# A two-layer encoder trunk (convolution, gated recurrence): small loads on GpSimd's queue or later, masks and lower bounds prepared in mid-run, first low parts on GpSimd

## The chip and the metric

One core of one Trainium2 chip. The metric is the device time of one execution in microseconds; the time before is 1019.38 us, the median of 3 runs (1018.51 to 1019.60). TensorE multiplies matrices, VectorE, ScalarE and GpSimd work on elements, and SyncE issues DMAs. Each engine works off its own queue in order; semaphores tie the queues together.

## What is computed

256 positions by 2048 channels, float32, two layers. Layer 0 is a gated convolution, layer 1 a bidirectional gated recurrence; both multiply their result by a gate and project it back.

```python
# layer 0
h = rms_norm(x, conv_norm)
a, b, z = split(h @ conv_w_in, 3)                    # w_in: 2048 x 6144
v = a * sigmoid(b)
v = depthwise_conv(v, conv_dw, width=31) + conv_dw_b
v = silu(layer_norm(v, conv_ln_g, conv_ln_b))
x = x + (v * silu(z)) @ conv_w_out                   # 2048 x 2048
# layer 1
h = rms_norm(x, hgrn_norm)
q, a_f, a_b, i, z = split(h @ hgrn_w_in, 5)          # 2048 x 10240
lb = cumsum(softmax(table over layers))              # one per direction; minus its first row
f = lb + (1 - lb) * sigmoid(a)                       # forget gate, k = (1 - lb) * sigmoid(-a)
o = forward and backward recurrence over 256 steps, 16 heads of 128
x = x + (rms_norm(o, o_norm) * silu(z)) @ hgrn_w_out
```

## The kernel before

**Weights.** Every product is done as three matmuls on a high and a low part of each operand (or two and a wide one): `hi*hi`, `hi*lo`, `lo*hi`. A list `plan` cuts the weights into blocks of 1 MB, 128 x 2048 values each. A block passes through three steps. `w_dma` (L109) loads it on SyncE's queue into one of 3 `raw` buffers; `w_split` (L122) lets ScalarE cast it to the high part `wh` (L134), and VectorE or GpSimd subtract that from `raw` to give the low part `wl` (L135); `w_next` (L139) hands it to the matmuls and keeps two splits and three loads ahead. There are 3 buffers of `wh` and `wl`. Blocks 0 to 47 are layer 0's input projection: blocks 0 to 7 are narrow (128 columns, all 2048 rows, a and b in turn for four column blocks), 8 to 31 are a and b of the column pairs 2 to 7, 32 to 47 are the gate z. The low part of blocks 4 to 47 is made by GpSimd, of all others by VectorE; blocks 0 to 3 are split in four pieces of 128x512.

**Start.** x is loaded, then one small vector, block 0 in four pieces, four vectors, block 1, five vectors, conv_dw (31 x 2048) and seven masks of 128 x 128, all on SyncE's queue (L256 to L276). The small ones land in `stage2`, as rows that TensorE transposes. ScalarE squares and sums x, VectorE makes a diagonal of the row norms, and `h0_gen` (L310) transposes and scales x by matmuls with that diagonal; `hilo` (L240) takes the high part on ScalarE and the low part on VectorE from PSUM. The 16 steps of `h0_gen` are interleaved with the first pass of matmuls (`pa` of block 0, L521). Behind that pass comes `vec_gen` (L335): it transposes the vectors and conv_dw, casts the masks to bytes, and computes the lower bounds `lb` and `oml = 1 - lb` of layer 1 in a chain of ten small VectorE operations with an exponential on ScalarE between them.

**Middle.** For each column pair `glu` multiplies a by the sigmoid of b on VectorE, then `conv_gen` (L404) runs 27 taps a block on VectorE and 4 on ScalarE and GpSimd, paced by estimated times against the matmuls (`run`, L233). `ln_gen` (L450) is the layer norm behind the last pair; the z blocks run beside it.

**Order.** What the program writes for one engine is ordered by a planner that simulates all engines: the instruction first in program order among those that it estimates to be ready goes first. So an instruction further down in the program can stand ahead of an earlier one in an engine's queue. The pool `pmm` has 4 slots of PSUM for the results of matmuls and for transposes.

Of the kernel before, what the change touches and what calls it, by code (L numbers as in the profile page):

```python
# [10 lines left out]
F32 = mybir.dt.float32  # L11
# [6 lines left out]
P = 128  # L18
S = 256
D = 2048  # L20
KB = D // P
CW = 31
# [6 lines left out]
NWD = D // WD  # L29
NKW = 4  # L30
AHEAD = 2
DV = 8
CHAIN0 = 2
ZPOS = 3
TK, TN = .654, .327
# [14 lines left out]
def trunk(ctx: ExitStack, tc: tile.TileContext, x, conv_norm, conv_w_in, conv_dw, conv_dw_b, conv_ln_g,  # L50
# [71 lines left out]
    def w_split():  # L122
        i = state["split"]
        if i >= len(plan):
            return
        raw = raws.pop(i)
        nk, ncol = raw.shape[1:]
        wh = wp.tile([P, nk, ncol], F32R, tag="wh", name=f"wh{i}", bufs=SPL + 1)
        wl = wp.tile([P, nk, ncol], F32R, tag="wl", name=f"wl{i}", bufs=SPL + 1)
        eng = G if 4 <= i < n_a and i % 8 != DV else V  # L130
        step = nk if i > 3 else 4
        for k in range(0, nk, step):
            sl = slice(k, k + step)
            A.copy(wh[:, sl, :], raw[:, sl, :])  # L134
            eng.tensor_tensor(out=wl[:, sl, :], in0=raw[:, sl, :], in1=wh[:, sl, :].bitcast(F32), op=ALU.subtract)  # L135
        splits[i] = (wh, wl)
        state["split"] = i + 1
# [95 lines left out]
    def run(gen, dt):  # L233
        for _ in gen:
            clock["pe"] += dt
            flush(clock["pe"])
            while bg and clock["bg"] <= clock["pe"]:
                clock["bg"] = max(clock["bg"], clock["pe"] - 2.0) + (pump() or clock["wait"])
# [22 lines left out]
    stage2 = big.tile([P, KB * S], F32, tag="yl", name="stage2")  # L261
    rows = stage2[:80, :2 * P].rearrange("q (a p) -> q a p", a=2)
    rows1, rows2 = rows[:, 0, :], rows[:65, 1, :]
    sync(rows1[:KB, :], conv_norm[0].rearrange("(a p) -> a p", p=P))
    w_dma()
    for i, v in enumerate((conv_dw_b[0], conv_ln_g[0], conv_ln_b[0], hgrn_norm[0])):
        sync(rows1[(i + 1) * KB:(i + 2) * KB, :], v.rearrange("(a p) -> a p", p=P))
    w_dma()
    for i, v in enumerate((lb_f[0], lb_b[0], lb_f[1], lb_b[1])):
        sync(rows2[i * KB:(i + 1) * KB, :], v.rearrange("(a p) -> a p", p=P))  # L270
    sync(rows2[64:65, :], o_norm)
    dwr = stage2[:CW, D:]
    sync(dwr, conv_dw[0])
    mask = cst.tile([P, len(LEVELS), P], U8, name="mask")
    mstage = stage2[:, 2 * P:(2 + len(LEVELS)) * P].rearrange("q (a p) -> q a p", p=P)
    sync(mstage, masks)  # L276

    ident = cst.tile([P, P], F32, name="ident")
    make_identity(nc, ident)
    ones = cst.tile([P, P], F32, name="ones")  # L280
    V.memset(ones, 1.0 / D)
    bcb = cst.tile([P, 1, S], F32, name="bcb")
# [49 lines left out]
    lb = cst.tile([P, 32], F32, name="lb")  # L332
    oml = cst.tile([P, 32], F32, name="oml")

    def vec_gen():  # L335
        tp = pmm.tile([P, 512], F32, tag="mm", name="tp_v1")
        nc.tensor.transpose(tp[:, :80], rows1, ident[:80, :80])
        nc.tensor.transpose(tp[:, 80:145], rows2, ident[:65, :65])
        V.tensor_copy(pvec[:, KB:], tp[:, KB:80])
        V.tensor_copy(pvec2, tp[:, 80:145])  # L340
        V.tensor_copy(mask, mstage)
        tp = pmm.tile([P, 512], F32, tag="mm", name="tp_dw")
        for k in range(KB):
            nc.tensor.transpose(tp[:, k * CW:(k + 1) * CW], dwr[:, k * P:(k + 1) * P], ident[:CW, :CW])
        V.tensor_copy(dw.rearrange("p k c -> p (k c)"), tp[:, :KB * CW])
        yield


        t0, t1 = pvec2[:, 0:32], pvec2[:, 32:64]
        lbw = cst.tile([P, 4, 32], F32, name="lbw")  # L350
        V.tensor_tensor(out=lbw[:, 0], in0=t0, in1=t1, op=ALU.max)
        V.tensor_tensor(out=lbw[:, 1], in0=t0, in1=lbw[:, 0], op=ALU.subtract)
        V.tensor_tensor(out=lbw[:, 2], in0=t1, in1=lbw[:, 0], op=ALU.subtract)
        A.activation(lbw[:, 1:3], lbw[:, 1:3], AF.Exp)
        V.tensor_tensor(out=lbw[:, 3], in0=lbw[:, 1], in1=lbw[:, 2], op=ALU.add)
        V.reciprocal(lbw[:, 3], lbw[:, 3])
        V.tensor_tensor(out=lbw[:, 1], in0=lbw[:, 1], in1=lbw[:, 3], op=ALU.mult)
        V.tensor_tensor(out=lbw[:, 2], in0=lbw[:, 2], in1=lbw[:, 3], op=ALU.mult)
        V.tensor_tensor(out=lb, in0=lbw[:, 1], in1=lbw[:, 2], op=ALU.add)
        V.tensor_tensor(out=lb, in0=lb, in1=lbw[:, 1], op=ALU.subtract)  # L360
        V.tensor_scalar(out=oml, in0=lb, scalar1=-1.0, scalar2=1.0, op0=ALU.mult, op1=ALU.add)
        yield


    yr = []
# [148 lines left out]
    for j in range(NCH):  # L514
        vb = vbuf[j % NV][:, :, PADW:PADW + S]
        sg = ca.tile([P, 2, S], F32, tag="sg", name=f"sg{j}", bufs=3)
        if j < NARROW:
            for u in range(2):
                pa = pmm.tile([P, S], F32, tag="mm", name=f"pa{j}_{u}")
                if j == 0 and u == 0:  # L520
                    for _ in ws_narrow(pa, hh, hl):  # L521
                        next(h0, None)
                    for _ in vec_gen():
                        pass
                else:
                    run(ws_narrow(pa, hh, hl), TN)
                pb = pmm.tile([P, S], F32, tag="mm", name=f"pb{j}_{u}")
                run(ws_narrow(pb, hh, hl), TN)
                A.activation(sg[:, u, :], pb, AF.Sigmoid)

                def glu(j=j, u=u, pa=pa, sg=sg, vb=vb):
# [17 lines left out]
                bg.append(ln_gen())  # L549

        later(LAG, glu)
    for j in range(NCH):
        pz = pmm.tile([P, 2, S], F32, tag="mm", name=f"pz{j}")
        run(ws_chunk(pz, hh, hl), TK)
# [288 lines left out]
```

## Time and profile before

| | us |
|---|---|
| median of 3 runs | 1019.38 |
| profiled execution | 1018.37 |
| its span, first to last instruction | 1016.6 |
| TensorE busy | 998.2 |
| VectorE busy | 753.7 |
| ScalarE busy | 511.3 |
| GpSimd busy | 243.8 |

An engine's busy time is what its instructions cover. Matmuls overlap: one of 256 columns lasts 0.28 us in the rows, and one starts every 0.12 us. A row of a view in order of time has the start in us from the start of the span, the busy time, the engine and line, the operation, `out<-in`, the shapes, a count where like ones were merged, and in brackets how long the engine stood idle ahead of it and who ended that. L12 is line 12 of the kernel. In the view by stretch each engine has its busy us and the number of its instructions; then come the granted clock, the mean busy share of the 16 DMA engines and GB/s. "Clock" is the granted clock of TensorE as a share of full speed.

### The profile page before, as it was taken

Reading aid. Unit: us, or ns where it says so; the run is one execution under the profiler, and the core shown is the slowest. Engines: PE = TensorE matmul, PEld = TensorE weight load, DVE = VectorE, ACT = ScalarE, POOL = GpSimd, SP = SyncE. Lnnn points to the kernel's source line nnn. Section 1 sums busy time; section 2 is a strip of 40 time slices with the busy share of each in tenths; the row PEclk is TensorE's granted clock in tenths of the full one; section 3 lists DMA queues with packets and bytes.
Section 4 is the critical chain, followed back from the end, with each engine's and each line's share of the span. In section 5 each row is a group of like instructions: output and inputs, shape, how many; then the busy total and the mean of one; then the engine's idle time right before and its main releaser. Section 6 shows DMA issues by size and latency. Waiting matters only on the chain.

```text
span 1016.6 us, 16064 instructions
## 1 busy us (share of the span) xinstructions
PE 998.2 (98%) x6625; PEld 883.9 (87%) x6625; DVE 753.7 (74%) x1214; ACT 511.3 (50%) x576; POOL 243.8 (24%) x99
## 2 busy tenths in 40 slices
PE   5999999999999999999999999999999999999998
PEld 5899999999997888888888888888888888887886
DVE  4687888888698655657877868778778786888552
ACT  6554554544565545454454555544555445454431
POOL 0399999999750000000000000000000000000000
PEclk9999999999999999999999999999999999999999
DMA  7755555555546555564454545555354555445461
GB/s 232 202 178 184 189 177 195 170 185 187 175 158 214 199 176 197 166 202 155 163 170 145 178 149 166 166 166 166 126 167 164 166 164 168 127 164 166 145 228 42
DMA packets 143995, 173.79 MB, mean 171 GB/s; under 512 B 2946, under 2 KB 109587, under 8 KB 143763
## 3 DMA queue, kind: packets, MB, share of 16 engines
q1 hardware_dynamic: 143922, 172.77, 52.4%
q8 instruction: 52, 0.85, 0.4%
q14 instruction: 21, 0.17, 0.0%
HBM read 170.66 MB, written 2.10 MB: 170 GB/s over the span
## 4 chain that ended last, share of the span: by engine, by line
PE 94%; DVE 2%; DMA 2%; SPq 1%; issue 0%; ACT 0%; DVEq 0%
PE psaf L172 6%; PE psab L172 6%; PE psq L172 6%; PE lv L682 4%; PE psab L174 3%; PE psaf L174 3%; PE psq L174 3%; PE psz L190 3%; PE pq L190 3%; PE psv L190 3%; PE po L191 3%; PE psv L191 3%; PE psz L191 3%; PE psz L192 3%; PE po L192 3%; PE psv L192 3%
## 5 line engine op out<-in xcount | busy, mean ns | idle before, releaser
L134 ACT CAST wh<-raw 128x2048 fp32r<-128x2048 f32 (+1 forms) x172 | 306.8, 1789 | 269.7 <-issue 52.6
L135 DVE TENSOR_TENSOR wl<-raw,wh 128x2048 fp32r<-128x2048 f32 (+1 forms) x128 | 266.8, 2090 | 114.2 <-ACT wh L134 112.6
L135 POOL TENSOR_TENSOR wl<-raw,wh 128x2048 fp32r<-128x2048 f32 x44 | 203.1, 4632 | 54.7 <-ACT wh L134 54.5
L426 DVE SCALAR_TENSOR_TENSOR acc<-vb,dw,acc 128x256 f32<-128x256 f32 x416 | 168.4, 481 | 12.0 <-ACT acc L401 10.7
L172 PE MATMUL psab<-hx,wh 128*128 128x512 f32 x256 | 92.8, 404 | 0.0
L172 PE MATMUL psaf<-hx,wh 128*128 128x512 f32 x256 | 92.8, 404 | 0.0
L172 PE MATMUL psq<-hx,wh 128*128 128x512 f32 x256 | 92.3, 402 | 0.0
L688 DVE TENSOR_TENSOR T<-T,pb 128x512 f32<-128x512 f32 x96 | 62.8, 686 | 15.9 <-PE lv L682 15.6
L158 PE MATMUL pz<-hx,wh 128*128 128x256 f32 x256 | 72.8, 285 | 0.0
L159 PE MATMUL pz<-hx,wh 128*128 128x256 f32 x256 | 72.7, 284 | 0.0
L160 PE MATMUL pz<-hx,wl 128*128 128x256 f32 x256 | 72.5, 283 | 0.0
L174 PE MATMUL psq<-hx,wl 128*128 128x256 f32 x256 | 72.2, 282 | 0.0
L174 PE MATMUL psab<-hx,wl 128*128 128x256 f32 x256 | 72.0, 281 | 0.0
L174 PE MATMUL psaf<-hx,wl 128*128 128x256 f32 x256 | 71.9, 281 | 0.0
L172 PEld LDWEIGHTS psaf<-hx,wh 128*128 128x128 f32 x256 | 48.1, 188 | 12.5
L172 PEld LDWEIGHTS psab<-hx,wh 128*128 128x128 f32 x256 | 48.1, 188 | 12.2
L172 PEld LDWEIGHTS psq<-hx,wh 128*128 128x128 f32 x256 | 48.1, 188 | 11.7
L662 ACT COPY kx<-T 128x512 f32<-128x512 f32 x56 | 37.0, 661 | 37.8 <-DVE T L688 37.7
L160 PE MATMUL pb<-hx,wl 128*128 128x256 f32 x192 | 54.4, 283 | 0.0
L158 PE MATMUL pa<-hx,wh 128*128 128x256 f32 x192 | 54.4, 283 | 0.0
L159 PE MATMUL pa<-hx,wh 128*128 128x256 f32 x192 | 54.4, 283 | 0.0
L158 PE MATMUL pb<-hx,wh 128*128 128x256 f32 x192 | 54.4, 283 | 0.0
(198 smaller groups left out, 2419.1 us busy)
## 6 DMA issues: line engine op xcount, KB each, us to landing
raw<-in_hgrn_w_in SPq DMA_DIRECT2D x80, 1024.0 KB, 5.1
raw<-in_conv_w_in SPq DMA_DIRECT2D x47, 1024.0 KB, 5.3
raw<-in_conv_w_out SPq DMA_DIRECT2D x16, 1024.0 KB, 5.2
raw<-in_hgrn_w_out SPq DMA_DIRECT2D x16, 1024.0 KB, 5.2
out<-ot SPq DMA_DIRECT2D x8, 256.0 KB, 2.4
xt<-in_x SPq DMA_DIRECT2D x1, 1024.0 KB, 5.1
xt<-in_x SPq DMA_DIRECT2D x2, 512.0 KB
raw<-in_conv_w_in SPq DMA_DIRECT2D x4, 256.0 KB, 7.9
```

What stands on the lines that cost most here:

```text
L134: A.copy(wh[:, sl, :], raw[:, sl, :])
L135: eng.tensor_tensor(out=wl[:, sl, :], in0=raw[:, sl, :], in1=wh[:, sl, :].bitcast(F32), op=ALU.subtract)
L158: mm(ps[:, j, :], lhsT=a, rhs=hi[:, k, :], start=(k == 0 and j == 0), stop=False)
L159: mm(ps[:, j, :], lhsT=a, rhs=lo[:, k, :], start=False, stop=False)
L160: mm(ps[:, j, :], lhsT=wl[:, kk, j * P:(j + 1) * P], rhs=hi[:, k, :], start=False, stop=(k == KB - 1 and j == 1))
L172: mm(ps[j].rearrange("p a s -> p (a s)"), lhsT=wh[:, kk, j * P:(j + 1) * P], rhs=hx[:, k].rearrange("p a s -> p (a s)"), start=(k == 0), s ...
L174: mm(ps[j][:, 0, :], lhsT=wl[:, kk, j * P:(j + 1) * P], rhs=hx[:, k, 0, :], start=False, stop=(k == KB - 1))
L190: mm(ps[t], lhsT=a, rhs=wh[:, kk, :], start=(k == 0), stop=False)
L191: mm(ps[t], lhsT=a, rhs=wl[:, kk, :], start=False, stop=False)
L192: mm(ps[t], lhsT=lo[:, k, t * P:(t + 1) * P], rhs=wh[:, kk, :], start=False, stop=(k == KB - 1))
L426: ins = V.scalar_tensor_tensor(out=accs[j, u], in0=vb[:, u, c:c + S], scalar=dw[:, k, c:c + 1], in1=accs[j, u], op0=ALU.mult, op1=ALU.add)
L688: V.tensor_tensor(out=tv, in0=tv, in1=pv, op=ALU.mult)
```

## The change

The loads of conv_norm, conv_dw, conv_dw_b, conv_ln_g, conv_ln_b and hgrn_norm are issued from GpSimd's queue, after the identity matrix is made there; on SyncE's queue blocks 0 and 1 follow x directly. The tables of the lower bounds, o_norm and the masks stay on SyncE, but are issued in the program behind the first pass, when the loads up to block 5 are written. `vec_gen` is cut in two: `vec_conv` (vectors of layer 0, conv_dw) is called behind the matmuls of block 1, `vec_rec` (masks, lower bounds) ahead of the z blocks. The low parts of the first two pieces of block 0 and of blocks 1 to 3 go to GpSimd. `DV` goes; its test was always true.

```diff
--- before.py
+++ after.py
@@ -29,7 +29,6 @@
 NWD = D // WD
 NKW = 4
 AHEAD = 2
-DV = 8
 CHAIN0 = 2
 ZPOS = 3
 TK, TN = .654, .327
@@ -127,10 +126,10 @@
         nk, ncol = raw.shape[1:]
         wh = wp.tile([P, nk, ncol], F32R, tag="wh", name=f"wh{i}", bufs=SPL + 1)
         wl = wp.tile([P, nk, ncol], F32R, tag="wl", name=f"wl{i}", bufs=SPL + 1)
-        eng = G if 4 <= i < n_a and i % 8 != DV else V
         step = nk if i > 3 else 4
         for k in range(0, nk, step):
             sl = slice(k, k + step)
+            eng = G if i < n_a and (i > 0 or k < 2 * step) else V
             A.copy(wh[:, sl, :], raw[:, sl, :])
             eng.tensor_tensor(out=wl[:, sl, :], in0=raw[:, sl, :], in1=wh[:, sl, :].bitcast(F32), op=ALU.subtract)
         splits[i] = (wh, wl)
@@ -261,22 +260,25 @@
     stage2 = big.tile([P, KB * S], F32, tag="yl", name="stage2")
     rows = stage2[:80, :2 * P].rearrange("q (a p) -> q a p", a=2)
     rows1, rows2 = rows[:, 0, :], rows[:65, 1, :]
-    sync(rows1[:KB, :], conv_norm[0].rearrange("(a p) -> a p", p=P))
-    w_dma()
-    for i, v in enumerate((conv_dw_b[0], conv_ln_g[0], conv_ln_b[0], hgrn_norm[0])):
-        sync(rows1[(i + 1) * KB:(i + 2) * KB, :], v.rearrange("(a p) -> a p", p=P))
-    w_dma()
-    for i, v in enumerate((lb_f[0], lb_b[0], lb_f[1], lb_b[1])):
-        sync(rows2[i * KB:(i + 1) * KB, :], v.rearrange("(a p) -> a p", p=P))
-    sync(rows2[64:65, :], o_norm)
-    dwr = stage2[:CW, D:]
-    sync(dwr, conv_dw[0])
     mask = cst.tile([P, len(LEVELS), P], U8, name="mask")
     mstage = stage2[:, 2 * P:(2 + len(LEVELS)) * P].rearrange("q (a p) -> q a p", p=P)
-    sync(mstage, masks)
-
+    dwr = stage2[:CW, D:]
+    small = G.dma_start
     ident = cst.tile([P, P], F32, name="ident")
     make_identity(nc, ident)
+    small(rows1[:KB, :], conv_norm[0].rearrange("(a p) -> a p", p=P))
+    w_dma()
+    w_dma()
+    small(dwr, conv_dw[0])
+    for i, v in enumerate((conv_dw_b[0], conv_ln_g[0], conv_ln_b[0], hgrn_norm[0])):
+        small(rows1[(i + 1) * KB:(i + 2) * KB, :], v.rearrange("(a p) -> a p", p=P))
+
+    def late_loads():
+        for i, v in enumerate((lb_f[0], lb_b[0], lb_f[1], lb_b[1])):
+            sync(rows2[i * KB:(i + 1) * KB, :], v.rearrange("(a p) -> a p", p=P))
+        sync(rows2[64:65, :], o_norm)
+        sync(mstage, masks)
+
     ones = cst.tile([P, P], F32, name="ones")
     V.memset(ones, 1.0 / D)
     bcb = cst.tile([P, 1, S], F32, name="bcb")
@@ -332,18 +334,20 @@
     lb = cst.tile([P, 32], F32, name="lb")
     oml = cst.tile([P, 32], F32, name="oml")
 
-    def vec_gen():
+    def vec_conv():
         tp = pmm.tile([P, 512], F32, tag="mm", name="tp_v1")
         nc.tensor.transpose(tp[:, :80], rows1, ident[:80, :80])
-        nc.tensor.transpose(tp[:, 80:145], rows2, ident[:65, :65])
         V.tensor_copy(pvec[:, KB:], tp[:, KB:80])
-        V.tensor_copy(pvec2, tp[:, 80:145])
-        V.tensor_copy(mask, mstage)
         tp = pmm.tile([P, 512], F32, tag="mm", name="tp_dw")
         for k in range(KB):
             nc.tensor.transpose(tp[:, k * CW:(k + 1) * CW], dwr[:, k * P:(k + 1) * P], ident[:CW, :CW])
         V.tensor_copy(dw.rearrange("p k c -> p (k c)"), tp[:, :KB * CW])
-        yield
+
+    def vec_rec():
+        tp = pmm.tile([P, 512], F32, tag="mm", name="tp_v2")
+        nc.tensor.transpose(tp[:, :65], rows2, ident[:65, :65])
+        V.tensor_copy(pvec2, tp[:, :65])
+        V.tensor_copy(mask, mstage)
 
 
         t0, t1 = pvec2[:, 0:32], pvec2[:, 32:64]
@@ -359,7 +363,6 @@
         V.tensor_tensor(out=lb, in0=lbw[:, 1], in1=lbw[:, 2], op=ALU.add)
         V.tensor_tensor(out=lb, in0=lb, in1=lbw[:, 1], op=ALU.subtract)
         V.tensor_scalar(out=oml, in0=lb, scalar1=-1.0, scalar2=1.0, op0=ALU.mult, op1=ALU.add)
-        yield
 
 
     yr = []
@@ -520,12 +523,13 @@
                 if j == 0 and u == 0:
                     for _ in ws_narrow(pa, hh, hl):
                         next(h0, None)
-                    for _ in vec_gen():
-                        pass
+                    late_loads()
                 else:
                     run(ws_narrow(pa, hh, hl), TN)
                 pb = pmm.tile([P, S], F32, tag="mm", name=f"pb{j}_{u}")
                 run(ws_narrow(pb, hh, hl), TN)
+                if j == 0 and u == 0:
+                    vec_conv()
                 A.activation(sg[:, u, :], pb, AF.Sigmoid)
 
                 def glu(j=j, u=u, pa=pa, sg=sg, vb=vb):
@@ -549,6 +553,7 @@
                 bg.append(ln_gen())
 
         later(LAG, glu)
+    vec_rec()
     for j in range(NCH):
         pz = pmm.tile([P, 2, S], F32, tag="mm", name=f"pz{j}")
         run(ws_chunk(pz, hh, hl), TK)
```

## Rows read from the trace of the kernel before

**Rows 1.** busy by stretch: stretch, length, PE, PEld, DVE, ACT, POOL, clock, DMA, GB/s
```profile
22.00:26.50 4.50, 4.31 (x36) 4.31 (x37) 2.76 (x7) 1.96 (x5) 0.00 (x0) 1.00 0.10 31
26.50:31.10 4.60, 2.24 (x21) 1.68 (x19) 1.48 (x6) 0.80 (x2) 0.00 (x0) 0.99 0.22 64
31.10:35.00 3.90, 3.90 (x22) 3.84 (x22) 2.75 (x7) 2.05 (x4) 0.00 (x0) 0.57 1.17 306
...
60.00:250.00 190.00, 190.00 (x1586) 190.00 (x1585) 160.61 (x401) 98.00 (x114) 188.75 (x72) 1.00 0.57 183
```

**Rows 2.** order of time, VectorE, start: start us, busy us, what [idle before]
```profile
24.60 0.48 DVE L242 SCALAR_TENSOR_TENSOR hx<-tp,pvec,hx 128x256 fp32r<-128x256 f32 x1 [0.66 <-ACT hx L241]
25.63 0.48 DVE L242 SCALAR_TENSOR_TENSOR hx<-tp,pvec,hx 128x256 fp32r<-128x256 f32 x1 [0.54 <-ACT hx L241]
29.54 0.63 DVE L341 CAST mask<-stage 128x896 uint8<-128x896 f32 x1 [3.42 <-DMA stage<-in_masks]
...
31.10 0.49 DVE L242 SCALAR_TENSOR_TENSOR hx<-tp,pvec,hx 128x256 fp32r<-128x256 f32 x1
...
32.20 0.18 DVE L352 TENSOR_TENSOR lbw<-pvec,lbw 128x32 f32<-128x32 f32 x1
...
33.60 2.50 DVE L135 TENSOR_TENSOR wl<-raw,wh 128x512 fp32r<-128x512 f32 x4 [1.12 <-ACT wh L134]
```

**Rows 3.** order of time, SyncE's queue, two issues
```profile
14.69 0.22 SPq L273 DMA_DIRECT2D stage<-in_conv_dw  x1
...
17.27 12.05 SPq L118 DMA_DIRECT2D raw<-in_conv_w_in  x1
```

**Rows 4.** order of time, ScalarE, two casts of weights
```profile
32.95 2.18 ACT L134 CAST wh<-raw 128x512 fp32r<-128x512 f32 x4 [1.89 <-DMA raw<-in_conv_w_in]
...
40.41 1.90 ACT L134 CAST wh<-raw 128x2048 fp32r<-128x2048 f32 x1
```

**Rows 5.** order of time, GpSimd, from its first low part on
```profile
42.39 4.63 POOL L135 TENSOR_TENSOR wl<-raw,wh 128x2048 fp32r<-128x2048 f32 x1 [40.79 <-ACT wh L134]
...
104.00 1.32 POOL L415 TENSOR_TENSOR prods<-prods 128x512 f32<-128x512 f32 x1
...
211.95 13.80 POOL L135 TENSOR_TENSOR wl<-raw,wh 128x2048 fp32r<-128x2048 f32 x3
...
235.77 4.61 POOL L135 TENSOR_TENSOR wl<-raw,wh 128x2048 fp32r<-128x2048 f32 x1
...
285.18 4.75 POOL L135 TENSOR_TENSOR wl<-raw,wh 128x2048 fp32r<-128x2048 f32 x1 [1.11 <-ACT wh L134]
```

**Rows 6.** order of time, TensorE, first passes and block 37
```profile
29.02 0.86 PE L344 MATMUL tp_dw<-ident,stage 31*128 31x31 f32 x11
...
31.50 0.58 PE L198 MATMUL pb<-hx,wh 128*128 128x256 f32 x1
...
34.23 0.39 PE L198 MATMUL pb<-hx,wh 128*128 128x256 f32 x1
...
39.02 0.28 PE L198 MATMUL pa<-hx,wh 128*128 128x256 f32 x1
...
240.62 0.28 PE L158 MATMUL pz<-hx,wh 128*128 128x256 f32 x1
```

**Rows 7.** waits of TensorE: us in total, times, longest
```profile
PE tp_v L293 <- DMA stage<-in_conv_norm: 9.8, 1, 9.8
```

**Rows 8.** order of time, VectorE, around and after pair 7's gate
```profile
214.66 0.69 DVE L545 TENSOR_TENSOR vb<-pa,sg 128x512 f32<-128x512 f32 x1 [2.72 <-ACT sg L542]
...
231.63 7.15 DVE L426 SCALAR_TENSOR_TENSOR acc<-vb,dw,acc 128x256 f32<-128x256 f32 x18 [2.42 <-ACT acc L401]
...
257.71 1.88 DVE L468 TENSOR_TENSOR y<-y,mu_ps 128x512 f32<-128x512 f32 x3 [4.03 <-PE mu_ps L454]
...
285.98 4.10 DVE L498 TENSOR_SCALAR y<-y,pvec 128x256 f32<-128x256 f32 x1
...
291.20 0.40 DVE L498 TENSOR_SCALAR y<-y,pvec 128x256 f32<-128x256 f32 x1
```

## The prediction

> **What bounds the kernel now.** I read the busy table by stretch first. From 60 to 250 us TensorE is busy 190.00 of 190.00 us, one matmul every 0.12 us (190.00 over 1586), at full clock [rows 1]; no edit can help there except by not hurting. What is left to win is at the start: in 26.50 to 31.10 TensorE is busy 2.24 of 4.60 us, and from 31.10 to 35.00 the granted clock is 0.57 of full speed, the lower of its two levels for most of it [rows 1]. Then I asked who holds TensorE there. VectorE's order of time [rows 2] shows it: it ends a low part at 26.11, then sits 3.42 us for the mask DMA, casts the mask at 29.54, and only then makes the last two low parts of the normalised input, the second at 31.10. The mask is not needed before layer 1; it stands in an in-order queue ahead of what TensorE needs. The third view is SyncE's queue and the DMA share [rows 3, 1]: conv_dw, 31 rows of 2048 values (248 KB), is issued at 14.69, and from 22.00 to 26.50 the 16 DMA engines are busy 0.10, near one engine of 16 (0.06). SyncE hangs 12.05 us in one weight issue from 17.27, and ScalarE waits for weight block 2 until 32.95 [rows 4]. One long-running transfer on about one engine holds up masks and weights behind it.
>
> A second limit hides under TensorE's: in 60 to 250 GpSimd is busy 188.75 of 190.00 [rows 1]. Its low part of block 4 starts at 42.39, that of block 37 ends at 240.38 (235.77 plus 4.61) [rows 5], and TensorE begins block 37 at 240.62, 35 blocks of 5.76 after block 2 at 39.02 [rows 6]. So GpSimd is 0.2 us ahead there (0.5 to the first matmul that takes the low part), and whatever makes it late shows as TensorE idle.
>
> **The change part by part.** I measure the start by when TensorE begins block 2, 39.02 now [rows 6].
>
> (a) Masks and bounds leave the start. The last low parts follow each other by 1.03 us (24.60 to 25.63) [rows 2]. Without the mask the last would end at 25.63 + 2 x 1.03 + 0.48 = 28.2 instead of 31.10 + 0.49 = 31.6: minus 3.4 us.
>
> (b) If the gap goes, so does the clock's drop: the 13 matmuls between 31.50 and 34.23 take 2.73 us [rows 6], at 0.12 each 1.56: minus 1.2. If a gap of like size stays elsewhere: 0.
>
> (c) The 17 transposes of the first vectors and of conv_dw now run in TensorE's gaps; they move behind pb of block 1, where no gap covers them. Eleven take 0.86, a step of 0.064 [rows 6]: plus 1.1. At best they fill gaps again: 0.
>
> (d) Weight block 2 comes earlier, because SyncE no longer passes conv_dw and the small vectors ahead of it. Its four casts (2.18 on ScalarE [rows 4]) can then go ahead of remaining high parts: 0 to plus 2.2, I take plus 1.1. Four low parts of a block leave VectorE (2.50 [rows 2]), which mattered only where VectorE held ScalarE up: 0 to minus 2.5, taken minus 0.6.
>
> (e) The PSUM slots of the two transposed vector tiles no longer stand between the first pass and the second, so matmuls of pb whose inputs are there may fill gaps: 0 to minus 4.3 (36 x 0.12); I take minus 1.5, a third of it, since the first pass leaves little room while it runs (TensorE busy 4.31 of 4.50 from 22.00 to 26.50 [rows 1]).
>
> Sum at the start: minus 3.4, 1.2, 0.6, 1.5, plus 1.1, 1.1: minus 4.5.
>
> (f) Six vectors go through GpSimd's queue. The trace has no such issue. The gain norm came through SyncE in time for TensorE to transpose it after a wait of 9.8 us from the start [rows 7]; it is needed by the first high part right behind the first casts. Below: an instant landing gains nothing, the square sums hold the start. Above: if it took as long as the longest issue of the start, 12.05 [rows 3], it would land near 14 and cost about 4. I take 0, by the nearest row, the same vector through SyncE. The five others are needed after block 1 only. SyncE's six late loads stand behind the weight issues up to block 5 and ahead of block 6, which TensorE wants only four blocks (23 us) after block 2; hidden, unless SyncE hangs again.
>
> (g) GpSimd takes 14 low parts of 128x512. Its add of that size takes 1.32 [rows 5], so 18.5 us in all, in a stretch where it does nothing now (it starts at 42.39). When does it reach block 4? If the casts of block 2 come only after the last high part, near 28.8, then 8 x 1.32 more make 39.5; if earlier, the cast of block 4 sets it, now at 40.41 [rows 4], then 4.5 earlier: 37.8 at its end. So block 4 starts 2.9 to 4.6 earlier; I take 3.8. With the 0.5 of lead, the later stretch can give TensorE 4.2 of its 4.5. If GpSimd were late here, all that is lost, one for one.
>
> (h) The moved preparation now stands in VectorE's queue just before the gate of block pair 7 (now 214.66), while GpSimd has low parts back to back. What this costs is shown by a row: at 285.98 the scale-and-shift of line 498, 0.40 when alone, takes 4.10 and ends at 290.08, as GpSimd's low part ends (285.18 + 4.75 = 289.93) [rows 8, 5]; 2 other such waits end the same way. So VectorE's tensor_scalar between SBUF tiles waits out a whole GpSimd instruction. Two of the moved operations are of like kind, SBUF to SBUF with one input: mask cast and oml. Each may wait 0 to 4.6, and the ten small ones at 0.18 [rows 2] and the cast at 0.63 add 2.5. Against 2.5 + 4.6 VectorE has idle 2.72 before that gate, 2.42 at 231.63 and 4.03 before 257.71 [rows 8]: most of it is covered. But the gate comes some 3.6 late, and behind it in ScalarE's queue stand a tap start, products and a weight cast that feeds GpSimd, whose lead is 0.2 to 0.5. I take plus 1.0, from 0 (covered) to 3. The two table loads that the exponential needs on ScalarE move there too; ScalarE is busy 98.00 of 190.00 [rows 1], no charge.
>
> A rule speaks against (h). The Trainium skill's page "SBUF — State Buffer", section "Who interferes with whom", says that a VectorE instruction in a two-port mode, or with two SBUF inputs while GpSimd reads SBUF, and a GpSimd instruction exclude each other for the whole instruction. The trace agrees for line 498; it has no case with two SBUF inputs. By it eight more of the moved operations would wait, which is the third rival.
>
> Total: minus 4.2 plus 1.0 is minus 3.2 on the profiled execution's 1018.37 (span 1016.6 and 1.8 around it): 1015.2. The median of the three runs, 1019.38, is 1.0 above that execution, so I state 1016.2.
>
> **The rivals.**
> 1. The start gives more: pb fills every gap (e at 4.3) and block 2 is cast early, block 4 starts at 36, (h) is covered. Gain 6 to 7: 1012.5. For it: DMA engines idle from 22 us on. Against: GpSimd's 0.2 us lead.
> 2. conv_dw clogs again. Now it goes out some 10 us earlier. If it again runs on about one engine, it shares that engine with x and the first weight blocks: 248 KB at one engine's share take about 10 us, half of it beside them. The first low parts then wait 2 to 4 us and eat most of (a): 1018.5 to 1020. For it: the 0.10 in rows 1. Against: another queue may spread it. The "DMA: Bandwidth & Descriptors" page of the Trainium skill (section "Why a DMA increments its semaphore by 16 and not by 1") says that GpSimd's queue gives some copies all 16 engines although 16 does not divide their rows; no run here shows that.
> 3. The other side: VectorE is blocked between GpSimd's low parts. Place: 212 to 240. If the mask cast, three small operations ahead of the exponential, and six behind it each wait for a GpSimd instruction, the first alone waits until 216.6 and the next until 221.3 (three low parts of 4.6 from 211.95 [rows 5]); the gate of pair 7 slips from 214.66 to about 222, and the weight cast behind it in ScalarE's queue with it. Then GpSimd itself starves, which lets the rest through. Low part 35, which now ends at 225.75 and is wanted at 229.1 (39.02 + 33 x 5.76), ends some 5.4 later, 2.0 too late, and 36 another 3: 5 us of TensorE idle, up to 12 if the second group is blocked as well, of which I take 6.5. That gives 1018.37 - 4.2 + 6.5 + 1.0 = 1021.7. It decides once the gate is later than about 220. For it: GpSimd's 188.75 of 190.00. Against: two-input operations are not seen to wait.
> 4. It does not do what it says: TensorE's start is held by the chain of high and low parts anyway (1.03 a step), (d) and (c) take what (a) gives, and (h) takes the rest: 1019.
>
> **How the numbers follow.** Forecast 0.44 (own range 1013.5 to 1018.5), rival 1 0.12, rival 2 0.10, rival 3 0.26, rival 4 0.08. 0.2% is 2.0 us, about what a measurement of this kernel can tell: faster is below 1017.4, slower above 1021.4. Faster: two thirds of the forecast (0.29), rival 1 and 0.01 of rival 2, 0.42. Slower: the upper part of rival 3 (0.20) and 0.04 of the others, 0.24. The same: 0.34. The range 1012 to 1023 leaves out a tenth at either end.
>
> **What would show it.** (a), (b): no VectorE wait for masks before 40 us, full clock at 31 to 35, block 2 begun near 34.5 instead of 39.02. (d): ScalarE not waiting for block 2. (f): conv_norm transposed by about 9.8. (g): GpSimd at block 4 near 38.5. (h): mask cast and oml longer than alone, and TensorE's idle from 212 to 260. I am wrong if TensorE begins block 2 later than 38, or if it idles more than 4 us between 212 and 260, or if the 128x512 low part on GpSimd takes far more than 1.32.

## The result and the profile after

The changed kernel takes 1024.19 us, the median of 5 runs (1023.29 to 1025.40); the kernel before, run beside it, 1018.97. The ratio is 1.0053, with a 95% interval of 1.0042 to 1.0065: slower by 5 us, where a gain of 3 was forecast. The profiled execution after took 1023.29, 4.9 us more than the one before (1018.37).

The view by stretch, of the same stretches of the start and of three in the middle (columns as in [rows 1]):

```profile
22.00:26.50 4.50, 2.64 (x20) 2.25 (x20) 2.20 (x5) 3.64 (x8) 4.50 (x5) 1.00 0.62 151
26.50:31.10 4.60, 4.60 (x39) 4.38 (x38) 1.93 (x4) 1.89 (x4) 3.52 (x3) 1.00 0.78 216
31.10:35.00 3.90, 3.90 (x33) 3.84 (x32) 0.49 (x2) 2.66 (x5) 1.56 (x2) 1.00 1.00 269
220.00:230.00 10.00, 9.80 (x82) 9.60 (x80) 10.00 (x18) 7.49 (x12) 5.95 (x2) 1.00 0.48 157
230.00:240.00 10.00, 7.18 (x55) 6.98 (x56) 10.00 (x26) 4.36 (x5) 9.84 (x6) 0.97 0.33 107
240.00:250.00 10.00, 10.00 (x75) 10.00 (x75) 10.00 (x26) 4.28 (x4) 9.92 (x5) 0.86 0.64 210
```

The hole from 26.50 to 31.10 and the fall of the clock behind it are gone, the DMA engines carry 0.62 where they carried 0.10 [rows 1]. But a hole has come at 22.00 to 26.50, and from 220 to 250, where TensorE had no gap, 212 matmuls ran in 30 us, where [rows 1] has 1586 in 190, about 250 in 30. In the last two of these stretches the granted clock is 0.97 and 0.86 besides. TensorE's waits name both places (us in total, times, longest; `hx` is the normalised input, `wl` a low part of the weights):

```profile
PE tp_v L295 <- DMA stage<-in_conv_norm: 7.9, 1, 7.9
PE tp L320 <- DVE diag L310: 3.8, 2, 1.9
PE pz L159 <- POOL wl L134: 3.0, 2, 2.5
PE pa L197 <- ACT hx L240: 1.7, 1, 1.7
...
PE pa L197 <- DVE pvec L340: 0.8, 1, 0.8
```

Where block 2 begins, in TensorE's order of time (the first row is for a comparison below):

```profile
27.16 1.05 PE L320 MATMUL tp<-diag,xt 128*128 128x128 f32 x8
...
39.13 0.38 PE L197 MATMUL pa<-hx,wh 128*128 128x256 f32 x1 [0.83 <-DVE pvec L340]
```

39.13 against 39.02 [rows 6]: the start has gained nothing. VectorE in order of time, three rows of the start and five of the middle:

```profile
12.97 1.00 DVE L310 TENSOR_SCALAR diag<-ident,ss 128x128 f32<-128x128 f32 x1
...
31.64 0.48 DVE L241 SCALAR_TENSOR_TENSOR hx<-tp,pvec,hx 128x256 fp32r<-128x256 f32 x1 [0.54 <-ACT hx L240]
37.31 1.63 DVE L350 CAST mask<-stage 128x896 uint8<-128x896 f32 x1 [5.18 <-DMA stage<-in_masks]
...
212.80 4.26 DVE L355 TENSOR_TENSOR lbw<-pvec 128x32 f32<-128x32 f32 x1
...
217.37 4.26 DVE L356 TENSOR_TENSOR lbw<-pvec,lbw 128x32 f32<-128x32 f32 x1
...
222.05 0.68 DVE L549 TENSOR_TENSOR vb<-pa,sg 128x512 f32<-128x512 f32 x1
...
225.59 0.18 DVE L364 TENSOR_TENSOR lb<-lb,lbw 128x32 f32<-128x32 f32 x1
...
226.08 4.22 DVE L365 TENSOR_SCALAR oml<-lb 128x32 f32<-128x32 f32 x1
```

The same small operation lasts 4.26 or 0.18. The gate of pair 7 stands behind two of the long ones, at 222.05 instead of 214.66 [rows 8]. GpSimd and ScalarE in order of time:

```profile
12.62 2.49 POOL L134 TENSOR_TENSOR wl<-raw,wh 128x512 fp32r<-128x512 f32 x2 [7.45 <-ACT wh L133]
...
39.05 4.62 POOL L134 TENSOR_TENSOR wl<-raw,wh 128x2048 fp32r<-128x2048 f32 x1 [0.60 <-ACT wh L133]
...
212.38 9.21 POOL L134 TENSOR_TENSOR wl<-raw,wh 128x2048 fp32r<-128x2048 f32 x2
225.64 4.62 POOL L134 TENSOR_TENSOR wl<-raw,wh 128x2048 fp32r<-128x2048 f32 x1 [4.05 <-ACT wh L133]
```
```profile
10.88 1.06 ACT L306 ACTIVATE stage<-xt 128x1024 f32<-128x1024 f32 x1 [1.51 <-DMA xt<-in_x]
...
15.28 0.47 ACT L240 ACTIVATE hx<-tp,pvec 128x256 fp32r<-128x256 f32 x1 [1.31 <-PE tp L320]
...
22.63 2.17 ACT L133 CAST wh<-raw 128x512 fp32r<-128x512 f32 x4
...
221.77 0.26 ACT L358 ACTIVATE lbw<-lbw 128x64 f32<-128x64 f32 x1 [5.93 <-DVE lbw L357]
...
223.67 1.89 ACT L133 CAST wh<-raw 128x2048 fp32r<-128x2048 f32 x1
```

Lay the rows over each other. GpSimd's two low parts from 212.38 end near 217.0 and 221.6. VectorE's two long operations end at 217.06 and 221.63, `oml` at 230.30 with GpSimd's next one (225.64 + 4.62 = 230.26). The six operations between them, at 0.18, fall into the 4.05 us in which GpSimd waits for ScalarE's cast. That cast, at 223.67, stands in ScalarE's queue behind the exponential of the chain, for which ScalarE sat idle 5.93 us until 221.77, and behind the first tap, which needs the late gate. So GpSimd starves, and TensorE waits 0.5 and 2.5 us for its low parts.

### The profile page after: what moved, and what is told of

The parts are those of the page before. It is cut to its first block, busy times and chain, and to the rows that moved or that the text cites. A ratio compares the mean times of both kernels' runs of the same rounds, so it can differ in the third digit from the quotient of the medians.

```text
span 1021.5 us, 16074 instructions
## 1 busy us (share of the span) xinstructions
PE 998.8 (98%) x6625; PEld 884.6 (87%) x6625; DVE 760.0 (74%) x1200; ACT 512.1 (50%) x577; POOL 265.0 (26%) x119
## 4 chain that ended last, share of the span: by engine, by line
PE 92%; DVE 3%; DMA 1%; ACT 1%; POOL 1%; issue 1%; SPq 0%; DVEq 0%; POOLq 0%; ACTq 0%
PE psaf L171 6%; PE psab L171 6%; PE psq L171 6%; PE lv L687 4%; PE psab L173 3%; PE psq L173 3%; PE psaf L173 3%; PE psz L189 3%; PE pq L189 3%; PE psv L189 3%; PE psv L190 3%; PE po L190 3%; PE psz L190 3%; PE psz L191 3%; PE po L191 3%; PE pq L190 3%
## 5 line engine op out<-in xcount | busy, mean ns | idle before, releaser
L134 DVE TENSOR_TENSOR wl<-raw,wh 128x2048 fp32r<-128x2048 f32 (+1 forms) x114 | 258.7, 2270 | 112.6 <-ACT wh L133 111.1
L134 POOL TENSOR_TENSOR wl<-raw,wh 128x2048 fp32r<-128x2048 f32 (+1 forms) x58 | 220.7, 3825 | 38.2 <-ACT wh L133 38.2
L159 PE MATMUL pa<-hx,wl 128*128 128x256 f32 x192 | 54.3, 283 | 0.0
```

The source lines that it names most:

```text
L159: mm(ps[:, j, :], lhsT=wl[:, kk, j * P:(j + 1) * P], rhs=hi[:, k, :], start=False, stop=(k == KB - 1 and j == 1))
```

## The experiments

Each was timed beside the kernel before, on one chip; 1 to 4, 5 to 8, 9 to 12 and 13 to 14 ran on four different chips, so across these groups the ratios are to be compared and not the us. "Block 2" is its first matmul in TensorE's order of time, in one profiled execution; before it is 39.02, after 39.13. The rows of the table are experiments 1 to 14.

| kernel | block 2 | us | ratio, 95% interval |
|---|---|---|---|
| change, chain of bounds in PSUM | 40.38 | 1018.81 | 1.0006 [0.9997, 1.0015] |
| before, preparation moved | 39.38 | 1022.98 | 1.0043 [1.0031, 1.0056] |
| change, conv_dw later | 38.65 | 1023.47 | 1.0048 [1.0034, 1.0061] |
| change, first low parts on VectorE | 40.41 | 1024.42 | 1.0053 [1.0040, 1.0065] |
| PSUM chain, mask cast on ScalarE | 40.40 | 1019.19 | 1.0005 [0.9996, 1.0014] |
| ... and block 0 and block 2's split mended | 36.83 | 1015.84 | 0.9977 [0.9968, 0.9986] |
| ... and conv_dw later: **all repairs** | 35.70 | 1014.65 | 0.9969 [0.9956, 0.9981] |
| before, preparation moved, PSUM, mask on ScalarE | 41.00 | 1019.42 | 1.0010 [1.0001, 1.0019] |
| all, block 0's low parts shared again | 36.16 | 1016.05 | 0.9979 [0.9970, 0.9988] |
| all, block 2 split early again | 36.96 | 1016.30 | 0.9980 [0.9971, 0.9989] |
| all, mask cast on VectorE again | 35.92 | 1014.93 | 0.9967 [0.9954, 0.9979] |
| all, small loads on SyncE's queue again | 40.73 | 1019.89 | 1.0015 [1.0006, 1.0023] |
| all, chain in SBUF again | 36.12 | 1020.30 | 1.0018 [1.0009, 1.0027] |
| all, blocks 1 to 3 on VectorE too | 38.00 | 1017.24 | 0.9994 [0.9985, 1.0003] |

The profiled executions fall into two groups. Take from each its time less the place of its block 2: before it is 1018.37 less 39.02, 979.35, after 1023.29 less 39.13, 984.16. The five kernels whose chain of bounds runs in the middle with its operands in SBUF (after, 2, 3, 4 and 13) have 983.9 to 984.8. The eleven others, before among them, have 978.9 to 979.4. So the start and the chain are two separate terms, and in these kernels the end moves by as much as block 2 does.

**1. The chain of bounds with at most one input in SBUF.** The operations stay where they are; one operand of each is kept in the PSUM tile of the transpose.

```diff
-V.tensor_tensor(out=lbw[:, 0], in0=t0, in1=t1, op=ALU.max)
+q = [tp[:, 128 + 32 * i:160 + 32 * i] for i in range(6)]
+V.tensor_tensor(out=q[0], in0=tp[:, 0:32], in1=t1, op=ALU.max)
...
-V.tensor_scalar(out=oml, in0=lb, ...)
+V.tensor_scalar(out=oml, in0=q[5], ...)
```

> The changed kernel, with the chain of the lower bounds kept partly in PSUM: every small VectorE operation of it has at most one SBUF input, and none goes from SBUF to SBUF. Place, order, exponential and table loads stay. Theory 1 (VectorE and GpSimd exclude each other where VectorE has two SBUF inputs or a scale-and-shift between SBUF tiles): the three operations of 4.2 us fall to 0.2, the gate of pair 7 comes back from 222.05 to about 215 to 217, TensorE's idle and slow clock between 220 and 250 (some 46 matmuls, 5.5 us) goes: 1018.5 to 1019.5. Theory 2 (the place costs it: ScalarE's queue held by the exponential and two table loads, whatever VectorE reads): 1023 to 1024.5.

VectorE in order of time, and the stretch around it (columns as in [rows 1]: GpSimd is busy 9.92 of 10.00 us):

```profile
214.07 0.19 DVE L357 TENSOR_TENSOR tp_v<-tp_v,pvec 128x32 f32<-128x32 f32 x1
...
215.84 0.69 DVE L553 TENSOR_TENSOR vb<-pa,sg 128x512 f32<-128x512 f32 x1 [0.61 <-ACT sg L550]
...
221.14 0.18 DVE L369 TENSOR_SCALAR oml<-tp_v 128x32 f32<-128x32 f32 x1
```
```profile
210.00:220.00 10.00, 10.00 (x86) 10.00 (x85) 8.08 (x26) 5.21 (x7) 9.92 (x5) 1.00 0.40 118
```

The same operations, with one copy more on VectorE and one on ScalarE, at the same place beside the same busy GpSimd, take 0.18 to 0.19 each (the reciprocal 0.35); TensorE waits for no low part there, and the time falls by 0.0047, 4.8 us. It is the place of the operands and not the work, nor the exponential and its table loads, which stayed (theory 2 is out). This kernel began block 2 at 40.38, 1.25 later than the change, with the same program there; see the last section.

**2. Before, with only the preparation moved.**

```diff
-        nc.tensor.transpose(tp[:, 80:145], rows2, ident[:65, :65])
-        V.tensor_copy(pvec2, tp[:, 80:145])
-        V.tensor_copy(mask, mstage)
+    vec_rec()                       # ahead of the z blocks, as in the change
```

> The kernel before, with one part of the change alone: the preparation for layer 1 is called ahead of the z blocks; all loads and all low parts stay as before. Theory 1: the same three waits of about 4.2 us stand between 212 and 231, 5 to 5.5 us are lost there, and the start changes by less than 1: 1023 to 1025. Rival (the loss of the change is bound up with the new start, for instance GpSimd's extra low parts that bring it late into the middle): 1017 to 1019.5.

```profile
212.97 4.28 DVE L353 TENSOR_TENSOR lbw<-pvec 128x32 f32<-128x32 f32 x1
...
226.27 4.22 DVE L363 TENSOR_SCALAR oml<-lb 128x32 f32<-128x32 f32 x1
```

VectorE's order of time shows the same stalls, TensorE's waits 3.1 us for GpSimd's low parts. This one edit makes the kernel before 1.0043 times as long: nearly the whole loss of the change. TensorE's clock stayed at 1.00 from 220 to 250 here, so the loss does not need the lower clock.

**3. The start: conv_dw later.** Its load is made to wait until x has been squared (a copy of 31 x 2 of the sums into its landing place); the four vectors behind it in the program have no such wait.

```diff
-    small(dwr, conv_dw[0])
+    A.copy(stage2[:CW, D - 1:D + 1], ss0[:CW, 1:3])
+    small(stage2[:CW, D:], conv_dw[0])
```

> The changed kernel, with conv_dw and four vectors held back on GpSimd's queue until x has been squared. Theory 3 (the start gives nothing because conv_dw now shares the DMA engines with x, so that the last half of x comes at 10.88 instead of 9.46): first high part near 14 instead of 15.28, block 2 begun 1 to 1.7 us earlier, 1022.5 to 1023.3. Rival (x is late for another reason, or the casts of block 2 and the mask hold the start anyway): 1024.

ScalarE, then VectorE:

```profile
9.22 1.06 ACT L303 ACTIVATE stage<-xt 128x1024 f32<-128x1024 f32 x1
```
```profile
12.04 2.35 DVE L311 TENSOR_SCALAR diag<-ident,ss 128x128 f32<-128x128 f32 x1
```

x is there 1.7 us earlier than in the change (10.88), so conv_dw's load beside x had cost that much. But the second diagonal matrix, a tensor_scalar from SBUF to SBUF, now falls under GpSimd's first two low parts as a whole and takes 2.35 where it took 0.29 before, so the first high part comes at 15.70, later than in the change. One repair uncovers the next; 0.5 us is left at block 2, less than expected, and the time does not tell the two kernels apart.

**4. The start: the first low parts on VectorE.**

```diff
-            eng = G if i < n_a and (i > 0 or k < 2 * step) else V
+            eng = G if 4 <= i < n_a else V
```

> The changed kernel, with the low parts of blocks 0 to 3 back on VectorE. Theory 3: GpSimd's low parts cost only the wait of the second diagonal (1.00 instead of 0.29), VectorE gets 14 x 0.62 us of work back between the low parts of the input: 1024 to 1026. Rival (GpSimd's first low parts hold the start up): 1021 to 1023.

```profile
13.81 0.28 DVE L310 TENSOR_SCALAR diag<-ident,ss 128x128 f32<-128x128 f32 x1
```

The diagonal matrix takes 0.28 again, but it begins at 13.81 instead of 12.97, behind two low parts of block 0 on VectorE, and is ready no earlier: 14.09 against 13.97. The first high part comes at 15.40 (15.28 in the change). Block 2 begins at 40.41, but TensorE's clock was low in this start (0.70 from 25 to 30), as in experiment 1. So the 1.28 between the two is not the price of the low parts; 14 has that on a start at full clock. No gain: the interval is that of the change.

**5. The masks' cast on ScalarE (with the chain in PSUM).**

```diff
-        V.tensor_copy(mask, mstage)
+        A.copy(mask, mstage)
```

> The kernel with the lower bounds' chain in PSUM, and besides the cast of the masks to bytes on ScalarE in place of VectorE. Theory A (the start lost part of its gain to the cast of the masks, which waits on VectorE for a low part on GpSimd and holds up the copy of the vectors' transpose behind it): block 2 begins 0.8 us earlier than with the cast on VectorE, TensorE waits for no copy of pvec there, and the time is about 0.8 us under the PSUM kernel's, some 1.000 of before. Rival B (the start is bound by the chain of x, its transposes and block 1's casts, and the cast stands beside it): block 2 begins no earlier, ratio 1.0005 as with the bounds in PSUM alone.

Block 2 at 40.40 against 40.38, ratio as in 1: no gain, as the rival had it. But the kernel of 1 does not show the wait of 0.83 us that the change has: its start was later by the low clock, and when TensorE came to block 2 the copy was already done. So this run can't price the cast's place; 11 has it on a start at full clock.

**6. Block 0 and block 2's split.**

```diff
-            eng = G if i < n_a and (i > 0 or k < 2 * step) else V
+            eng = G if 0 < i < n_a else V
...
-        while state["split"] < min(len(plan), i + 1 + SPL):
+        far = i + 1 + SPL - (i == 0)      # the loads likewise: far + RAW
+        while state["split"] < min(len(plan), far):
```

> As the one before, and besides all four low parts of block 0 on VectorE (blocks 1 to 3 stay on GpSimd), and block 2's split is begun with block 1's use, not with block 0's. Theory A: the second diagonal matrix takes 0.3 us in place of 1.0, as GpSimd's low parts begin after it; block 2's casts no longer stand ahead of half of the high parts; together 1 to 2 us less at the start than with the masks' cast moved alone: block 2 begins at 36.5 to 38, ratio 0.998 to 0.999. Rival B: the four low parts on VectorE stand ahead of its own low parts of x and give back what the diagonal matrix gains, block 2 begins at 38 to 39.5, ratio about 1.000.

Both edits together: block 2 at 36.83, ratio 0.9977, so rival B's time is out. Its mechanism is there all the same: the diagonal matrix stands behind two low parts on VectorE, begins at 13.97, and the first high part comes at 15.57 (15.31 in 5). By the rows the gain is the split's: block 2's casts stand between the high parts, TensorE's wait of 1.8 us for a high part is gone, and with it the low clock. Of the 3.57 us, about 1.25 are the clock's (last section), which leaves about 2.3 for the casts.

**7. All repairs: conv_dw later as well.**

> As the one before, and besides the load of conv_dw and of four vectors held until x has been squared, with conv_dw's load last. Theory A (each thing that stood beside the transposes took its part of the start's gain): x's last half is squared by 9.5 us in place of 10.9 and the second diagonal matrix is there 1.4 us earlier, since it is no longer blocked by GpSimd; block 2 begins at 35 to 37, and the time is 3 us under before's, ratio 0.997. Rival B (what bounds the start is the alternation of TensorE, ScalarE and VectorE over the 16 transposed blocks, and the wait for weights behind it): x comes earlier, block 2 begins at 38 or later all the same, ratio 0.999 to 1.001.

VectorE and TensorE in order of time:

```profile
13.03 0.28 DVE L312 TENSOR_SCALAR diag<-ident,ss 128x128 f32<-128x128 f32 x1
```
```profile
35.70 0.38 PE L198 MATMUL pa<-hx,wh 128*128 128x256 f32 x1
```

3.3 us earlier than before, and the time is 3.3 us less (1014.65 against 1017.99): this version beats both kernels. What the start gives reaches the end one for one; the prediction had 4.2 of 4.5.

**8. Before, with the preparation moved and mended.** The edits of 2, 1 and 5.

> The kernel before with one thing moved: the transpose, the masks' cast (on ScalarE) and the lower bounds' chain go to the gate projections, and the chain is kept in PSUM. The loads and the low parts stay as before. Theory A (two inputs in SBUF were the whole loss of this part): no loss in the middle, VectorE's copies at the start no longer wait for the masks, which come last on SyncE's queue at 29.5; only ScalarE's cast of them does, and it stands ahead of the last two high parts. If ScalarE waits there as VectorE did, the start gains nothing: ratio 1.000. If the masks land before that cast is reached, block 2 begins up to 3 us earlier: ratio 0.997. Rival B (the preparation costs something in the middle even without the blocked operations): ratio 1.002 or above.

ScalarE, and the view by stretch:

```profile
29.71 0.94 ACT L348 CAST mask<-stage 128x896 uint8<-128x896 f32 x1 [3.26 <-DMA stage<-in_masks]
```
```profile
30.00:40.00 10.00, 8.93 (x55) 8.64 (x56) 6.45 (x11) 6.89 (x12) 0.00 (x0) 0.66 1.04 279
```

The loss in the middle is gone (0.0033 less than in 2). The start isn't won: the planner puts the cast early here too, though it stands ahead of the z blocks in the program, ScalarE waits for the masks where VectorE did, and the clock falls. So moving the preparation gains nothing by itself while the loads stay; 12 shows what the loads' queue is worth.

**9 to 12. Each repair taken back from 7.** Four kernels: block 0's low parts as in the change; `far` without its `- (i == 0)`; the cast with `V.tensor_copy`; and `small = sync`.

> The kernel that was faster by 3.3 us (all repairs), with one repair taken back: block 0's low parts are again two on GpSimd and two on VectorE, as in the change. Theory A (GpSimd's low parts beside VectorE's diagonal matrix and its own low parts): the second diagonal matrix takes 1.0 to 2.4 us again, the first high part comes at about 15.5 in place of 14.6, and block 2 begins 0.7 to 1.5 us later than 35.7: 1015.3 to 1016.1, ratio 0.998. Rival B (it is hidden by the order of VectorE, whose own low parts stood ahead of the diagonal matrix anyway): block 2 begins within 0.4 us of 35.7, ratio 0.997.

> The kernel with all repairs, with another one taken back: block 2's split is begun with block 0's use again, so ScalarE's four casts of it (2.17 us together) stand in one piece ahead of nine high parts. Theory A (the casts delay the transposes by their whole length, as TensorE has no other work then): TensorE waits 1.7 us for a high part near 25, block 2 begins 1.5 to 2.2 us later than 35.7, ratio 0.9985 to 0.999. Rival B (block 1's matmuls fill the gap): under 0.7 us later, ratio 0.997 to 0.9975.

> The kernel with all repairs, with a third one taken back: the cast of the masks is on VectorE again, where the order puts it ahead of the copies of conv_norm's companions and of conv_dw. Theory A (VectorE waits there for the masks' transfer and then for a low part on GpSimd, and two tiles of PSUM come free late): TensorE waits up to 0.8 us before block 2, which begins 0.5 to 1 us later than 35.7, ratio 0.9975 to 0.998. Rival B (block 2 waits for no tile of PSUM here): same start, ratio 0.997.

> The kernel with all repairs, with the queue changed: conv_norm, conv_dw and the four vectors are issued by SyncE again in place of GpSimd, at the same place in the program, conv_dw after x has been squared. Theory A (it is GpSimd's queue, beside SyncE's, that keeps the small loads from the weights): SyncE issues no weights while it waits for the square and while the 31 rows go out, block 2's weights come after 30, the clock falls, and block 2 begins at 38 to 40, ratio 0.9995 to 1.001. Rival B (only the time of the load mattered, not its queue): block 2 begins within 0.7 us of 35.7, ratio 0.9965 to 0.9975.

Block 0's low parts shared, VectorE:

```profile
11.71 2.40 DVE L312 TENSOR_SCALAR diag<-ident,ss 128x128 f32<-128x128 f32 x1
```

Block 2's casts early, ScalarE and TensorE's waits:

```profile
21.56 2.18 ACT L133 CAST wh<-raw 128x512 fp32r<-128x512 f32 x4 [0.54 <-DMA raw<-in_conv_w_in]
```
```profile
PE pa L197 <- ACT hx L240: 0.8, 1, 0.8
```

Small loads on SyncE's queue: ScalarE, TensorE's wait, the queue itself, and the stretches:

```profile
30.07 0.62 ACT L133 CAST wh<-raw 128x512 fp32r<-128x512 f32 x1 [4.74 <-DMA raw<-in_conv_w_in]
```
```profile
PE pa L198 <- ACT hx L241: 4.6, 1, 4.6
```
```profile
14.22 15.63 SPq L117 DMA_DIRECT2D raw<-in_conv_w_in  x3
```
```profile
20.00:30.00 10.00, 6.48 (x54) 6.10 (x52) 3.40 (x8) 2.88 (x7) 2.26 (x2) 0.97 0.35 99
30.00:40.00 10.00, 8.88 (x57) 8.77 (x58) 1.19 (x3) 5.51 (x11) 8.89 (x8) 0.69 0.93 251
```

Shared low parts cost 0.46 us at block 2, early casts 1.26, both under what theory A expected; the ratios are 0.0010 and 0.0011 above 7's, with intervals that overlap its own. The mask's place is worth 0.2 us at block 2 and nothing in time. The queue of the six small loads is worth 5.03 us at block 2, a little more than theory A took: SyncE waits 2.6 us for the square of x before it issues conv_dw, the next three weight issues behind it take 15.63 us, block 2's weights reach ScalarE at 30.07, TensorE waits 4.6 us for a high part that stands behind their cast, and the clock falls, as before the change.

**13, 14. Two conditions.** The chain in SBUF again, on top of all repairs; and blocks 1 to 3 on VectorE as well (`4 <= i < n_a`).

> The kernel with all repairs of the start, with the chain of the lower bounds in SBUF again, as in the change. Theory A (the two losses are separate: the chain costs about 5 us in the middle whatever the start does, and the early start gives GpSimd no lead that would cover it, since GpSimd is busy without a gap): two operations of the chain take over 4 us each, TensorE waits 2.5 to 5 us for GpSimd's low parts, 1018.5 to 1020, ratio 1.001 to 1.002. Rival B (a start 3 us earlier gives GpSimd a lead that covers the stall): ratio 0.9975 to 0.999, and TensorE waits under 1.5 us for GpSimd.

> The kernel with all repairs, with the low parts of blocks 1 to 3 on VectorE too, so none of the small ones is on GpSimd. Theory A (the move of these low parts to GpSimd is worth little by itself: VectorE has room at the start once the masks are gone from it, and GpSimd's start of block 4 is set by ScalarE's cast): block 2 begins 0 to 1 us later than 35.7, ratio 0.997 to 0.998. Rival B (the 2.5 us of low parts of block 1 hold up VectorE's low parts of x, each of which holds ScalarE and TensorE): block 2 begins 1.5 to 3 us later, ratio 0.9985 to 1.000.

The chain in SBUF, VectorE and TensorE's waits:

```profile
209.80 4.20 DVE L357 TENSOR_TENSOR lbw<-pvec 128x32 f32<-128x32 f32 x1
...
214.32 4.26 DVE L358 TENSOR_TENSOR lbw<-pvec,lbw 128x32 f32<-128x32 f32 x1
```
```profile
PE pz L160 <- POOL wl L134: 3.0, 2, 2.5
```

Blocks 1 to 3 on VectorE, VectorE and TensorE's waits:

```profile
18.09 2.50 DVE L134 TENSOR_TENSOR wl<-raw,wh 128x512 fp32r<-128x512 f32 x4 [0.47 <-ACT wh L133]
```
```profile
PE pa L198 <- ACT hx L241: 1.2, 1, 1.2
```

The chain costs 0.0049 again: the two losses are separate, and an early start buys no lead for GpSimd that could pay for the stall. Low parts of blocks 1 to 3 on VectorE cost 2.30 us at block 2 and 0.0025 in time, as rival B had it, so this part of the change is a gain, once block 0 is left out of it.

## Why the prediction was wrong

Two sums failed. The first is the start: minus 4.5 forecast, plus 0.1 measured. The second is (h): plus 1.0 forecast, 5.2 measured. VectorE's first low part behind the z blocks, block 48's, starts 5.3 later, of which the start has 0.1. Before, then after:

```profile
305.13 2.27 DVE L135 TENSOR_TENSOR wl<-raw,wh 128x2048 fp32r<-128x2048 f32 x1
```
```profile
310.43 2.27 DVE L134 TENSOR_TENSOR wl<-raw,wh 128x2048 fp32r<-128x2048 f32 x1
```

The profiled execution is 4.9 longer: 0.1 and 5.2, less 0.4 behind that. Of the 5.2, TensorE's named waits are 3.0; the lower clock behind them has a part of the rest, which no run isolates.

(h) is the step that turned the sign. It read from line 498 that a tensor_scalar between SBUF tiles waits out GpSimd, and charged the mask's cast and `oml` alone; the operations with two inputs it left at 0.18 because the trace had none beside GpSimd. It also charged nothing for the exponential, at which ScalarE sat 5.93 us because the blocked chain came late. Experiments 1, 2 and 13 show that the chain's operands are the whole loss, and the rows that two of its eight two-input operations take 4.26 each, besides the 4.22 of `oml` that (h) had allowed for. The Trainium skill's page "SBUF — State Buffer", section "Who interferes with whom", which the prediction quoted as the rival, is borne out: two SBUF inputs on VectorE wait while GpSimd reads SBUF (4.26 against 0.18), one SBUF and one PSUM input does not (0.19 in experiment 1). Rival 3, at 0.26, had this mechanism, place and price: the gate near 222 (222.05), 5 us of TensorE idle by the first group. The second group, for which it took 1.5 more, fell into GpSimd's own idle time. Its 1021.7 is too low because it, too, counted on the start.

At the start the rows give each step a size; (e) is what is left over, so the sum closes by itself and proves nothing. Block 2 begins where the last low part ends plus what follows it.

- (a) Right as a mechanism: no wait for the masks stands ahead of the last low part. Its minus 3.4 stands in the sum below; other steps took it back, and that low part ends at 32.12 (31.59 before). (b) Right: clock 1.00 from 31.10 to 35.00. Its 13 matmuls are 12 steps in the rows, 0.1 us.
- (c) Right: 16 transposes in 1.18 us behind pb, forecast 1.1.
- (d) Mis-sized. Block 2's casts stood ahead of the high parts in full, 2.17 where 1.1 was taken; TensorE waited 1.7 for a high part. Experiment 6 gives about 2.3 for it, 10 only 1.26 on the mended start. The relief of VectorE (0.6) doesn't show in the change; with the other steps mended it is worth 2.30 (14).
- (f) Failed, 0 forecast and plus 1.7 measured: the first high part comes at 15.28 instead of 13.55. conv_norm itself landed in time (TensorE's wait 7.9 against 9.8 [rows 7]), but x came 1.4 us later (10.88 against 9.46), which experiment 3 puts down to conv_dw's load beside it. The diagonal matrix then waited 0.7 for GpSimd's low parts (1.00 against 0.29); with these on VectorE it was ready no earlier while x was late (4, 6), and 0.8 earlier once x was early (13.31 in 7, 14.11 in 9). The late x is a mild form of rival 2, which had set the loss at 2 to 4.
- (e) About right: pb's matmuls began at 30.03 in the gaps; what is left over in the sum for it is minus 1.3, forecast minus 1.5.
- The masks' cast was charged to the middle. The planner put it in the start, behind (a)'s low parts, where it waited for a low part on GpSimd and TensorE for it: 0.8 in the rows of the change. On the mended start it costs 0.2 (11).

Minus 3.4, 1.2 and 1.3, plus 1.2, 2.2, 1.7 and 0.8 is zero. VectorE's rows at 12.97 and 37.31 show the very wait that (h) describes, at places where the prediction had not looked for it: it priced the wait where the preparation went, and not where the low parts went.

(g) was right in the main: GpSimd's small low parts took 1.25, and block 4 started at 39.05 (forecast 38.5). Its 3.8 and the lead of 0.5 make 4.3, not 4.2. The lead it gave was gone by pair 7, where GpSimd's low parts begin at 212.38 (211.95 before [rows 5]), and 13 shows that it pays for nothing.

## What to carry to other kernels

Before small work is moved into a stretch where GpSimd has no gap, count its VectorE operations that read two operands from SBUF, or copy and scale from SBUF to SBUF: here each that met a GpSimd instruction lasted until that ended, up to 4.28 us. And count what waits for the chain in the other queues. The cure here was not another place but one operand in PSUM, 4.8 us for an edit of some fifteen lines. And when a wait is removed from an in-order chain, size what is next in each queue for the same chain: three smaller things of 0.8 to 2.2 us, and 1.2 of transposes, ate the whole gain. Taken back one by one from a mended start they cost less (0.2 to 1.3), so the sizes of such steps don't add up from one start to another.

## What the runs showed that was not expected

- conv_dw, 31 rows and 248 KB, landed 7.6 us after its issue on GpSimd's queue (median 9.5 for the quarters of block 0 beside it); on SyncE's queue the weight issues behind it took 12.05 [rows 3] and, three together, 15.63 us. As far as times go that agrees with what rival 2 quoted from the Trainium skill's page "DMA: Bandwidth & Descriptors", section "Why a DMA increments its semaphore by 16 and not by 1"; no run here counts the engines of one transfer.
- The blocked operations of the chain end within 0.1 us of the GpSimd instruction beside them, and their start isn't delayed in the records. A long small operation is the mark to look for, not an idle gap.
- The start stands on the edge of the clock's fall. With the same program there, in one profiled execution each, the change kept the full clock (eight 128-column matmuls in 1.05, above), and the kernel of experiment 1 did not; its granted clock from 20 to 30 was 0.84, in TensorE's order of time:

```profile
28.47 1.91 PE L320 MATMUL tp<-diag,xt 128*128 128x128 f32 x8
```

Ahead of both lies a wait of about 1.7 us for a high part. Experiments 4 and 5 show the lower clock too. That is 1.25 us of block 2's place that no edit made, so a difference of that size at the start says nothing unless the granted clock is the same.
